# A two-layer hybrid block: shorter triangular inverse, silu in pieces, norm chains raised in priority, and instruction order from the scheduler's timeline model

## The chip, the cores and the metric

The kernel runs on one core of one Trainium2 chip, in one launch. The metric is the device time of an execution in microseconds (us). Runs of the kernel before took 1651.51, 1644.26 and 1647.09 us; the median is 1647.09 us.

## The reference, cut to what matters

Two layers work on 256 tokens of x and 256 tokens of ctx, 1024 wide. The second layer needs only x at its end.

```python
for l in range(DEPTH):                                  # DEPTH = 2
    mod_x = silu(c) @ w_mod[l] + b_mod[l]               # six shifts, scales, gates; same for ctx
    h_x = modulate(rms_norm(x, norm1_g[l]), sh1_x, sc1_x)
    y_x, y_c = hybrid_mixer(h_x, h_c, ...)              # three branches, then @ w_o
    x = x + gt1_x * y_x
    h_x = modulate(rms_norm(x, norm2_g[l]), sh2_x, sc2_x)
    x = x + gt2_x * conv_ffn(h_x, w_up[l], conv_ffn_w[l], w_down[l])
    # ctx the same, in layer 0 alone
```

The mixer's branches are a spatial gating unit (a), differential softmax attention (b) and a gated delta rule (c). The last one works on chunks of 64 tokens in both directions: it solves a unit lower triangular system per chunk and head, and then runs a scan over four chunks of ctx and four of x:

```python
u = triangular_solve(I + a, v * beta, lower=True)
w = triangular_solve(I + a, kb * exp(G), lower=True)
def step(state, blk):
    v_new = u_c - w_c @ state
    o_c   = qd_c @ state + in_c @ v_new
    state = state * gt_c + kt_c^T @ v_new
```

## The kernel before, in words

Activations lie transposed in SBUF, features on the partitions and 512 columns (ctx, then x) along the free side; in layer 1 most products take the 256 columns of x alone (`c0 = 256`). Every large product is made of three fp32r matmuls per 128 by 128 block of weights: a weight block comes in by a DMA on SyncE's queue (`wload`, L269, or `first_load`, L301), ScalarE rounds it to fp32r (`wh`, L237), VectorE takes the rest (`wl`, L219), and TensorE multiplies high by high, low by high and high by low (`mm3`, L240 is the matmul line of all helpers). Names in the profile are the outputs: `pqkv`, `ptm`, `pu`, `pj`, `pg`, `pbr`, `pwo`, `pup` and `pdn` are such products. `pu`, `ptm`, `pj`, `pg` and `pbr` are independent of the branches' small steps, and can stand between them.

The order of the program: `start` (the first modulation rows and the first norm), `norm_end` or `norm_halves` (norm and modulation into `hh` and `hl`), the mixer, its last product `wo` (`pwo`), a norm, the feed-forward layer (`pup`, `pdn`), a norm, and again for layer 1. I call the norm between `wo` and the feed-forward layer of layer 0 boundary B, that between the layers boundary C, and the one before the last feed-forward layer boundary D. `norm_halves` treats x and then ctx: sums of squares (`pss`), a reciprocal root of ten small VectorE steps (`rsqv`, `rs`, `rsqt`), its broadcast by TensorE (`pb`), and for eight blocks a product `xn`, then `hh` on ScalarE and `hl` on VectorE. The other modulation rows are made beside all this by `mod` (L467): 80 DMAs of 512 KB (`wmt`, L478), one or two VectorE products with a sum each (`mj` and `wmt`, L483), by the silu of the condition `scb` (one ScalarE step over 2048 columns); `more` (L490) issues the next of them at fixed points of the layer's code.

Branch c: `gdn_solve` (L1210) inverts 32 by 32 blocks on VectorE in 31 steps of two operations (`sT`, `sL`), transposes the result twice (`sLC`, and `sLR` by way of a ScalarE copy `sLt`), makes the off-diagonal parts on TensorE (`pZ`, `pU`, tiles of 32 rows), and ScalarE copies all into `U` (L1257, L1279), which VectorE then scales. `gdn_step` (L1285) is one scan step: `pkS` (state times keys), `rhs` on VectorE, `pV` (times U), `vn` on VectorE in one or two forms, `pq` and `pgo` where an output is wanted, `pS`, and four times two `gS` updates on VectorE, from which the next `pkS` starts. These matmuls use 64 rows or 64 columns of the array. `gdn_out` turns the result (`pgT`) and VectorE multiplies it into `z`. Branch a: `pj` and a gelu give `gv`, which `pmix` multiplies by the gating weights `sguwb`, loaded on ScalarE's queue (L734). Branch b: scores `psc`, a softmax, `paT` (transposes), a copy `aT`, `po`, a norm of `on` after four heads, `poT`.

What order the instructions stand in on each engine is not written out: a list scheduler of the framework takes the program's operations with priorities (`tc.high_priority(offset=AHEAD)` raises them) and a model of the machine's timing, and gives each engine its queue, which runs strictly in that order.

Of the kernel before, what the change touches and what calls it, by code (L numbers as in the profile page):

```python
# [173 lines left out]
class _Kernel:  # L174
# [175 lines left out]

    def run(self):
        nc = self.nc
        self.ahead, self.late, self.alt = {}, [], 0
        xf, N = self.start()
        xsrc = self.a["xT"]
        for l in range(L):
            last = l == L - 1
            if l > 0:
                self.load_par(l)
            hh, hl = self.norm_halves(N) if last else self.norm_end(N, self.first)  # L360
            c0 = 256 if last else 0
            if not last:
                self.mods = self.mod()
            xf, N = self.mixer(l, hh, hl, xsrc, c0)
            hh, hl = self.norm_end(N) if last else self.norm_halves(N)
            N = self.ffn(l, hh, hl, xf, c0)
            if not last:
                xsrc = self.dp.tile([128, 8, NT], F32, tag="xs", name="xs")
                for j in range(2):
                    nc.scalar.dma_start(out=xsrc[:, 4 * j:4 * j + 4], in_=xf.t[j])  # L370
        for m0, m1 in ((0, 4), (4, 6), (6, 7), (7, 8)):
            nc.sync.dma_start(out=self.out[:, m0:m1], in_=xf.t[m0 // 4][:, m0 % 4:(m1 - 1) % 4 + 1, 256:512])
# [94 lines left out]
    def mod(self):  # L467


        nc = self.nc  # L470
        sb = self.cp.tile([128, 2, 1024], F32, tag="scb", name="scb")
        nc.sync.dma_start(out=sb, in_=self.a["cB"])
        self.act(sb, sb, AF.Silu)
        for n in range(80):
            l, j = (0, 16 + n) if n < 32 else (1, n - 32)
            vs = (0, 1) if l == 0 or j < 16 else (1,)
            w = self.wp.tile([128, 1024], F32, tag="wm", name="wmt", bufs=1)
            nc.sync.dma_start(out=w, in_=self.a["wmt"][n])  # L478
            if n % 4 == 0:
                m4 = self.small("m4", [128, 4, 2], bufs=2)  # L480
            for v in vs:
                o = w if v else self.tmp("mj", [128, 1024], BF16)
                nc.vector.scalar_tensor_tensor(out=o, in0=w, scalar=1.0, in1=sb[:, v], op0=ALU.mult, op1=ALU.mult,  # L483
                                               accum_out=m4[:, n % 4, v:v + 1])
            if n % 4 == 3:
                self.add(self.modv[l][:, j - 3:j + 1, vs[0]:], m4[:, :, vs[0]:],
                         self.P(l, "bmod", j - 3, 4).unsqueeze(2).to_broadcast([128, 4, len(vs)]))
            yield

    def more(self, n=1):  # L490
        for _ in range(n):
            next(self.mods, None)

    def mod_first(self, order):
        for g, h in order:
# [43 lines left out]
    def norm_halves(self, N):  # L539
# [6 lines left out]
        for v, cs in ((1, slice(256, 512)), (0, slice(0, 256))):  # L546
# [7 lines left out]
            for k in range(8):  # L554
                self.mul(xn[:, k, cs], xn[:, k, cs], pb[:, cs])
                sh = mv[:, s + k, v:v + 1]
                self.act(hh[:, k, cs], xn[:, k, cs], AF.Identity, bias=sh)
                self.stt(hl[:, k, cs], xn[:, k, cs], sh, hh[:, k, cs].bitcast(F32), ALU.add, ALU.subtract)
        self.rest = iter(())
        return hh, hl  # L560

# [67 lines left out]
    def mixer(self, l, hh, hl, xsrc, c0):  # L629
# [32 lines left out]
        if c0 == 0:  # L662
            p = [self.bank("pg"[m % 2], "pwo") for m in (6, 7)]
            w = [self.tiles(self.a["wo"][l, m], 0, 8) for m in (6, 7)]
            for i, v in self.ends(p, w, _Two(yh), _Two(yl)):
                self.resid(l, 16, 6 + i, xf, p[i], 0, 0.5, (v,))
                self.norm_add(N, 6 + i, v)
        return xf, N

    def resid(self, l, s, m, xf, p, c0, scale, vs=None):  # L670
# [539 lines left out]
    def gdn_solve(self, g):  # L1210
# [18 lines left out]
            self.sub(Lm[:, j + 1:, :m], Lm[:, j + 1:, :m], tv)  # L1229
        LC = self.tp.tile([128, 32, 32], F32, tag="t4a", name="sLC", bufs=1)  # L1230
        nc.vector.transpose(LC.rearrange("p i t -> p (i t)"), Lf)
        Lt = self.tp.tile([128, 32, 32], F32, tag="t4c", name="sLt", bufs=1)
        self.act(Lt, Lm.rearrange("p i c -> p c i"), AF.Copy)
        LR = self.tp.tile([128, 32, 32], F32, tag="t4b", name="sLR", bufs=1)
        nc.vector.transpose(LR.rearrange("p i t -> p (i t)"), Lt.rearrange("p c i -> p (c i)"))
        Z = self.tp.tile([128, 32, 32], F32, tag="t4c", name="sZ", bufs=1)
        Af = A.rearrange("p f t y -> p f (t y)")
        for hb in range(2):
            pz = self.bank("g", "pZ")
# [12 lines left out]
        for a in range(2):  # L1252
            for y in range(2):
                src = LCv if a == y else LRv
                for b in range(2):
                    r = slice(64 * a + 32 * b, 64 * a + 32 * b + 32)
                    self.act(U[r, :, y, :, 32 * b:32 * b + 32], src[r, :, y], AF.Copy)  # L1257
                b = 1 if a == y else 0
                r = slice(64 * a + 32 * b, 64 * a + 32 * b + 32)
                nc.gpsimd.memset(U[r, :, y, :, 32 - 32 * b:64 - 32 * b], 0.0)  # L1260
        for hb in range(2):
# [13 lines left out]
            for a in range(2):  # L1275
                for y in range(2):
                    b = 0 if a == y else 1
                    r = slice(64 * a + 32 * b, 64 * a + 32 * b + 32)
                    self.act(U[r, 2 * hb:2 * hb + 2, y, :, 32 - 32 * b:64 - 32 * b], pv[r, :, y], AF.Copy)  # L1279
        for t in range(4):  # L1280
            Ut = U[:, t].rearrange("p y h i -> p (y h) i")
            self.mul(Ut, Ut, g["r1"][:, t].unsqueeze(2).to_broadcast([128, 8, 64]))
# [88 lines left out]
    def ffn(self, l, hh, hl, xf, c0):  # L1371
        nc = self.nc
        n = NT - c0
        for hf in range(2):
# [49 lines left out]
            if ps:  # L1424
# [2 lines left out]
                    w[i] += self.tiles(self.a["wdn"][l, hf, 6 + i][:, k0:k0 + kn].rearrange("p k m -> p (k m)"), k0, kn)  # L1427
                fht, flt = _Two(fh), _Two(fl)
                for i, v in self.ends(ps, w, fht, flt):
                    self.resid(l, 40, 6 + i, xf, ps[i], 0, 1.0, (v,))  # L1430
                    self.norm_add(N, 6 + i, v)
        return N if l + 1 < L else None


# [25 lines left out]
```

## Time and profile before

| | us |
|---|---|
| median of three runs | 1647.09 |
| the profiled execution | 1642.39 |
| its span, first to last instruction | 1640.6 |
| TensorE busy | 1583.4 |
| VectorE busy | 1207.0 |
| ScalarE busy | 767.9 |

The profiled execution is 1.8 us longer than its span, and 4.7 us (0.3%) under the median of the runs. "Busy" adds the time in which an engine ran at least one instruction; a pipelined engine can be busy and still deliver less than it could. The granted clock is TensorE's, 1.00 for its upper level.

### The profile page before, as it was taken

What the parts mean: (1) busy time and instruction counts of PE and PEld (TensorE: products, weight loads), DVE (VectorE), ACT (ScalarE), POOL (GpSimd) and SP (SyncE); (2) the same over time, 40 slices, a digit from 0 to 9 for tenths busy, and PEclk for the clock granted to TensorE, in tenths of its full rate; (3) what the DMA queues carried; (4) which work ended last, traced back from release to release, by engine and by line L of the source; (5) the groups of instructions that cost most, each with busy time, mean ns of one, the idle gap of its engine ahead of it and who ended that gap; (6) DMA issues with size and microseconds to landing.
All of it is one profiled execution on the core that took longest, in us unless ns stands there. A gap on an engine that the chain in (4) does not pass through costs nothing.

```text
span 1640.6 us, 27599 instructions
## 1 busy us (share of the span) xinstructions
PE 1583.4 (97%) x10664; PEld 1346.9 (82%) x10664; DVE 1207.0 (74%) x2831; ACT 767.9 (47%) x1455; POOL 6.6 (0%) x16
## 2 busy tenths in 40 slices
PE   5999999999999998999999999999999999989999
PEld 3777977876788887888888887888878799989998
DVE  5649977788764457999778876659777776788685
ACT  3654461156532333544234443654723754556563
POOL 0000000000000000000000000000000000000000
PEclk9999989999999998999999999999999999989999
DMA  8313321142343433454566565221222246545655
GB/s 340 132 60 110 107 66 53 65 125 69 100 145 94 150 93 101 128 171 160 166 203 201 191 195 182 78 92 53 70 64 83 86 144 223 186 132 180 191 181 154
DMA packets 65283, 218.22 MB, mean 133 GB/s; under 512 B 7552, under 2 KB 13696, under 8 KB 63232
## 3 DMA queue, kind: packets, MB, share of 16 engines
q1 hardware_dynamic: 63280, 208.70, 39.9%
q10 hardware_dynamic: 1872, 7.77, 1.3%
q8 instruction: 83, 1.36, 0.3%
q14 instruction: 48, 0.39, 0.1%
HBM read 213.29 MB, written 3.15 MB: 132 GB/s over the span
## 4 chain that ended last, share of the span: by engine, by line
PE 83%; DVE 7%; ACT 4%; DMA 2%; issue 2%; ACTq 0%; DVEq 0%
PE pup L240 21%; PE pg L240 12%; PE pdn L240 10%; PE pqkv L240 7%; PE pbr L240 6%; PE ptm L240 4%; PE pwo L240 4%; PE pu L240 2%; PE psc L240 2%; PE pj L240 2%; PE pS L240 2%; ACT U L237 1%; DMA wmt<-in_wmt_dram 1%; PE pkS L240 1%; PE po L240 1%
## 5 line engine op out<-in xcount | busy, mean ns | idle before, releaser
L237 ACT ACTIVATE wh<-wr 128x512 fp32r<-128x512 f32 (+1 forms) x594 | 366.7, 622 | 432.1 <-PE pdn L240 91.1
L219 DVE TENSOR_TENSOR wl<-wr,wh 128x512 fp32r<-128x512 f32 (+1 forms) x592 | 399.4, 680 | 156.8 <-ACT wh L237 154.1
L240 PE MATMUL pup<-hh,wh 128*128 128x256 f32 (+1 forms) x720 | 242.3, 337 | 2.2 <-ACT hh L237 2.1
L240 PE MATMUL pup<-hh,wl 128*128 128x256 f32 (+1 forms) x720 | 241.4, 336 | 0.0
L240 PE MATMUL pup<-hl,wh 128*128 128x256 f32 (+1 forms) x720 | 240.3, 335 | 0.0
L240 PEld LDWEIGHTS pup<-hh,wh 128*128 128x128 f32 x720 | 139.1, 193 | 16.8 <-ACT hh L237 2.9
L240 PEld LDWEIGHTS pup<-hh,wl 128*128 128x128 f32 x720 | 139.1, 193 | 13.0
L240 PEld LDWEIGHTS pup<-hl,wh 128*128 128x128 f32 x720 | 138.4, 193 | 13.1
L240 PE MATMUL pg<-hh,wh 128*128 128x512 f32 (+1 forms) x384 | 131.0, 341 | 0.1
L240 PE MATMUL pg<-hh,wl 128*128 128x512 f32 (+1 forms) x384 | 130.4, 339 | 0.2 <-DVE wl L219 0.2
L240 PE MATMUL pg<-hl,wh 128*128 128x512 f32 (+1 forms) x384 | 130.2, 339 | 0.0
L240 PE MATMUL ptm<-wh,hl 128*128 128x256 f32 x448 | 130.2, 291 | 0.0
L240 PE MATMUL ptm<-wl,hh 128*128 128x256 f32 x448 | 129.6, 289 | 0.3 <-DVE wl L219 0.3
L240 PE MATMUL ptm<-wh,hh 128*128 128x256 f32 x448 | 129.4, 289 | 0.0
L234 DVE SCALAR_TENSOR_TENSOR fcv<-pup,par,fcv 128x510 f32<-128x510 f32 (+1 forms) x176 | 107.3, 612 | 26.2 <-ACT fcv L237 26.1
L240 PE MATMUL pdn<-fh,wh 128*128 128x256 f32 (+1 forms) x366 | 121.0, 330 | 0.7 <-ACT fh L237 0.7
L240 PE MATMUL pdn<-fl,wh 128*128 128x256 f32 (+1 forms) x366 | 120.6, 330 | 0.7 <-DVE fl L219 0.7
L240 PE MATMUL pdn<-fh,wl 128*128 128x256 f32 (+1 forms) x366 | 120.7, 330 | 0.0
L483 DVE SCALAR_TENSOR_TENSOR wmt<-wmt,scb 128x1024 f32<-128x1024 f32 x80 | 97.7, 1221 | 23.1 <-DMA wmt<-in_wmt_dram 22.6
L240 PEld LDWEIGHTS ptm<-wh,hh 128*128 128x128 f32 x448 | 86.6, 193 | 2.7 <-issue 2.0
L240 PEld LDWEIGHTS ptm<-wl,hh 128*128 128x128 f32 x448 | 86.6, 193 | 2.5 <-issue 1.7
L240 PEld LDWEIGHTS ptm<-wh,hl 128*128 128x128 f32 x448 | 86.7, 194 | 2.1 <-issue 1.7
(332 smaller groups left out, 3223.1 us busy)
## 6 DMA issues: line engine op xcount, KB each, us to landing
wmt<-in_wmt_dram SPq DMA_DIRECT2D x80, 512.0 KB, 3.6
wr<-in_wup_dram SPq DMA_DIRECT2D x80, 512.0 KB, 3.9
wr<-in_wfm_dram SPq DMA_DIRECT2D x78, 512.0 KB, 3.5
wr<-in_wtm_dram SPq DMA_DIRECT2D x32, 512.0 KB, 3.6
wr<-in_wdn_dram SPq DMA_DIRECT2D x32, 512.0 KB, 3.9
wr<-in_wbr_dram SPq DMA_DIRECT2D x24, 512.0 KB, 3.6
wm<-in_wmod_dram SPq DMA_DIRECT2D x8, 1024.0 KB, 11.0
wr<-in_wo_dram SPq DMA_DIRECT2D x16, 512.0 KB, 3.5
```

The source lines that it names most:

```text
L219: self.nc.vector.tensor_tensor(out=out, in0=a, in1=b, op=op)
L234: self.nc.vector.scalar_tensor_tensor(out=out, in0=a, scalar=s, in1=b, op0=op0, op1=op1)
L237: self.nc.scalar.activation(out, a, f, bias=bias, scale=scale, **k)
L240: self.nc.tensor.matmul(out, lhsT, rhs, start=start, stop=stop, **k)
L483: nc.vector.scalar_tensor_tensor(out=o, in0=w, scalar=1.0, in1=sb[:, v], op0=ALU.mult, op1=ALU.mult, accum_out=m4[:, n % 4, v:v + 1])
```

## The change

- The scheduler is told to work with its other model of the machine (`schedule_with_timeline_sim=True`), so that the order on every engine is made anew.
- `norm_halves` and the residual and norm sums of the last two output blocks of `wo` and of `pdn` are raised in priority; the `wmt` products that `more` issues after a `norm_halves` are told to issue after its last `hl`.
- The silu of `scb` is made in four pieces of 512 columns.
- In the solve the copy `sLt` is dropped and `sLR` is transposed straight from the strided view of `sL`; half of the copies into `U` go from ScalarE to VectorE.

```diff
--- before.py
+++ after.py
@@ -350,19 +350,27 @@
 
     def run(self):
         nc = self.nc
-        self.ahead, self.late, self.alt = {}, [], 0
+        self.ahead, self.late, self.alt, self.after = {}, [], 0, None
         xf, N = self.start()
         xsrc = self.a["xT"]
         for l in range(L):
             last = l == L - 1
             if l > 0:
                 self.load_par(l)
-            hh, hl = self.norm_halves(N) if last else self.norm_end(N, self.first)
+            if last:
+                with self.tc.high_priority(offset=AHEAD):
+                    hh, hl = self.norm_halves(N)
+            else:
+                hh, hl = self.norm_end(N, self.first)
             c0 = 256 if last else 0
             if not last:
                 self.mods = self.mod()
             xf, N = self.mixer(l, hh, hl, xsrc, c0)
-            hh, hl = self.norm_end(N) if last else self.norm_halves(N)
+            if last:
+                hh, hl = self.norm_end(N)
+            else:
+                with self.tc.high_priority(offset=AHEAD):
+                    hh, hl = self.norm_halves(N)
             N = self.ffn(l, hh, hl, xf, c0)
             if not last:
                 xsrc = self.dp.tile([128, 8, NT], F32, tag="xs", name="xs")
@@ -470,7 +478,10 @@
         nc = self.nc
         sb = self.cp.tile([128, 2, 1024], F32, tag="scb", name="scb")
         nc.sync.dma_start(out=sb, in_=self.a["cB"])
-        self.act(sb, sb, AF.Silu)
+        for v in range(2):
+            for i in range(2):
+                s = sb[:, v, 512 * i:512 * i + 512]
+                self.act(s, s, AF.Silu)
         for n in range(80):
             l, j = (0, 16 + n) if n < 32 else (1, n - 32)
             vs = (0, 1) if l == 0 or j < 16 else (1,)
@@ -488,8 +499,9 @@
             yield
 
     def more(self, n=1):
-        for _ in range(n):
-            next(self.mods, None)
+        with self.tc.issue_after(self.after) if self.after is not None else ExitStack():
+            for _ in range(n):
+                next(self.mods, None)
 
     def mod_first(self, order):
         for g, h in order:
@@ -555,7 +567,9 @@
                 self.mul(xn[:, k, cs], xn[:, k, cs], pb[:, cs])
                 sh = mv[:, s + k, v:v + 1]
                 self.act(hh[:, k, cs], xn[:, k, cs], AF.Identity, bias=sh)
-                self.stt(hl[:, k, cs], xn[:, k, cs], sh, hh[:, k, cs].bitcast(F32), ALU.add, ALU.subtract)
+                self.after = self.nc.vector.scalar_tensor_tensor(
+                    out=hl[:, k, cs], in0=xn[:, k, cs], scalar=sh, in1=hh[:, k, cs].bitcast(F32), op0=ALU.add,
+                    op1=ALU.subtract).ins
         self.rest = iter(())
         return hh, hl
 
@@ -663,8 +677,9 @@
             p = [self.bank("pg"[m % 2], "pwo") for m in (6, 7)]
             w = [self.tiles(self.a["wo"][l, m], 0, 8) for m in (6, 7)]
             for i, v in self.ends(p, w, _Two(yh), _Two(yl)):
-                self.resid(l, 16, 6 + i, xf, p[i], 0, 0.5, (v,))
-                self.norm_add(N, 6 + i, v)
+                with self.tc.high_priority(offset=AHEAD):
+                    self.resid(l, 16, 6 + i, xf, p[i], 0, 0.5, (v,))
+                    self.norm_add(N, 6 + i, v)
         return xf, N
 
     def resid(self, l, s, m, xf, p, c0, scale, vs=None):
@@ -1229,11 +1244,9 @@
             self.sub(Lm[:, j + 1:, :m], Lm[:, j + 1:, :m], tv)
         LC = self.tp.tile([128, 32, 32], F32, tag="t4a", name="sLC", bufs=1)
         nc.vector.transpose(LC.rearrange("p i t -> p (i t)"), Lf)
-        Lt = self.tp.tile([128, 32, 32], F32, tag="t4c", name="sLt", bufs=1)
-        self.act(Lt, Lm.rearrange("p i c -> p c i"), AF.Copy)
-        LR = self.tp.tile([128, 32, 32], F32, tag="t4b", name="sLR", bufs=1)
-        nc.vector.transpose(LR.rearrange("p i t -> p (i t)"), Lt.rearrange("p c i -> p (c i)"))
-        Z = self.tp.tile([128, 32, 32], F32, tag="t4c", name="sZ", bufs=1)
+        LR = self.tp.tile([128, 32, 32], F32, tag="t4c", name="sLR", bufs=1)
+        nc.vector.transpose(LR, Lm.rearrange("p i c -> p c i"))
+        Z = self.tp.tile([128, 32, 32], F32, tag="t4b", name="sZ", bufs=1)
         Af = A.rearrange("p f t y -> p f (t y)")
         for hb in range(2):
             pz = self.bank("g", "pZ")
@@ -1254,7 +1267,10 @@
                 src = LCv if a == y else LRv
                 for b in range(2):
                     r = slice(64 * a + 32 * b, 64 * a + 32 * b + 32)
-                    self.act(U[r, :, y, :, 32 * b:32 * b + 32], src[r, :, y], AF.Copy)
+                    if b == 0:
+                        self.act(U[r, :, y, :, 0:32], src[r, :, y], AF.Copy)
+                    else:
+                        nc.vector.tensor_copy(U[r, :, y, :, 32:64], src[r, :, y])
                 b = 1 if a == y else 0
                 r = slice(64 * a + 32 * b, 64 * a + 32 * b + 32)
                 nc.gpsimd.memset(U[r, :, y, :, 32 - 32 * b:64 - 32 * b], 0.0)
@@ -1276,7 +1292,10 @@
                 for y in range(2):
                     b = 0 if a == y else 1
                     r = slice(64 * a + 32 * b, 64 * a + 32 * b + 32)
-                    self.act(U[r, 2 * hb:2 * hb + 2, y, :, 32 - 32 * b:64 - 32 * b], pv[r, :, y], AF.Copy)
+                    if a == 0:
+                        self.act(U[r, 2 * hb:2 * hb + 2, y, :, 32 - 32 * b:64 - 32 * b], pv[r, :, y], AF.Copy)
+                    else:
+                        nc.vector.tensor_copy(U[r, 2 * hb:2 * hb + 2, y, :, 32 - 32 * b:64 - 32 * b], pv[r, :, y])
         for t in range(4):
             Ut = U[:, t].rearrange("p y h i -> p (y h) i")
             self.mul(Ut, Ut, g["r1"][:, t].unsqueeze(2).to_broadcast([128, 8, 64]))
@@ -1427,8 +1446,9 @@
                     w[i] += self.tiles(self.a["wdn"][l, hf, 6 + i][:, k0:k0 + kn].rearrange("p k m -> p (k m)"), k0, kn)
                 fht, flt = _Two(fh), _Two(fl)
                 for i, v in self.ends(ps, w, fht, flt):
-                    self.resid(l, 40, 6 + i, xf, ps[i], 0, 1.0, (v,))
-                    self.norm_add(N, 6 + i, v)
+                    with self.tc.high_priority(offset=AHEAD):
+                        self.resid(l, 40, 6 + i, xf, ps[i], 0, 1.0, (v,))
+                        self.norm_add(N, 6 + i, v)
         return N if l + 1 < L else None
 
 
@@ -1452,7 +1472,7 @@
         arrays[f"in_{n}_dram"] = v
         aps[n] = nc.dram_tensor(f"in_{n}_dram", v.shape, mybir.dt.from_np(v.dtype), kind="ExternalInput").ap()
     out = nc.dram_tensor("out_0_dram", (128, 8, SEQ), F32, kind="ExternalOutput").ap()
-    with tile.TileContext(nc) as tc:
+    with tile.TileContext(nc, schedule_with_timeline_sim=True) as tc:
         body(tc, aps, out)
     r = run_bass_kernel_spmd(nc, [arrays], core_ids=[0])
     y = np.asarray(r.results[0]["out_0_dram"])
```

What the new order does shows at three places. The first is TensorE's queue in the second half of layer 0's scan: `ptm` are matmuls of a large product that nothing in the scan waits for, the others belong to a scan step. Before:

```order
L240 MATMUL pV_2885<-rhs_2880,U_1312 64x128 x4
L240 MATMUL pq_2897<-gS_2466,qT_616 64x128 x7
L240 MATMUL ptm1_3226<-wh_3233,hh_124 128x256
L240 MATMUL ptm1_3226<-wh_3233,hl_125 128x256
L240 MATMUL ptm1_3226<-wl_3234,hh_124 128x256
L240 MATMUL ptm1_3226<-wh_3229,hh_124 128x256
L240 MATMUL ptm1_3226<-wh_3229,hl_125 128x256
L240 MATMUL ptm1_3226<-wl_3230,hh_124 128x256
L240 MATMUL ptm1_3226<-wh_3229,hh_124 128x256
L240 MATMUL pgo_2906<-vn_2894,inT_1043 64x128 x8
L240 MATMUL pS_2919<-vn_2894,ktok_1041 128x128 x4
L240 MATMUL pS_2928<-vn_2894,ktok_1041 128x128 x4
```

And the steps of the changed kernel at the same place:

```order
L240 MATMUL ptm1_3381<-wl_3447,hh_124 128x256
L240 MATMUL pkS_2742<-gS_2467,kT_188 64x128 x8
L240 MATMUL pV_2756<-rhs_2751,U_1310 64x128 x2
L240 MATMUL pq_2768<-gS_2467,qT_616 64x128 x8
L240 MATMUL pV_2756<-rhs_2751,U_1310 64x128 x6
L240 MATMUL pgo_2777<-vn_2765,inT_1043 64x128 x8
L240 MATMUL pS_2789<-vn_2765,ktok_1041 128x128 x4
L240 MATMUL pS_2798<-vn_2765,ktok_1041 128x128 x4
L240 MATMUL pkS_2807<-gS_2467,kT_188 64x128 x8
L240 MATMUL pV_2821<-rhs_2816,U_1310 64x128 x2
L240 MATMUL pq_2833<-gS_2467,qT_616 64x128 x8
L240 MATMUL pV_2821<-rhs_2816,U_1310 64x128 x6
```

Before, each part of a step has matmuls of `ptm` (or of `pu`) behind it in the queue; now the four last steps of layer 0 (from `pkS_2742` on) follow each other with none between them, and so do, but for 22 matmuls of `pj` in the last, five of layer 1.

The second place is TensorE's queue at the end of branch b and the output of branch c in layer 0 (`pgT` turns a result of the scan; `pbr` and `pg` are matmuls of large products). Before:

```order
L1362 MATMUL pgT_4807<-cst0_77,go_2488 128x128 x4
L240 MATMUL pbr_4613<-yal_4304,wh_4605 128x512
L240 MATMUL pbr_4613<-yah_4303,wh_4605 128x512
L240 MATMUL pbr_4613<-yah_4303,wl_4606 128x512
L240 MATMUL pbr_4613<-yal_4304,wh_4605 128x512
L240 MATMUL pg_4627<-hh_124,wh_4630 128x512
L240 MATMUL pg_4627<-hh_124,wl_4631 128x512
L240 MATMUL pg_4627<-hl_125,wh_4630 128x512
L240 MATMUL pg_4627<-hh_124,wh_4630 128x512
L240 MATMUL pg_4627<-hh_124,wl_4631 128x512
L240 MATMUL pg_4627<-hl_125,wh_4630 128x512
L1362 MATMUL pgT_4816<-cst0_77,go_2546 128x128 x4
```

And now:

```order
L922 MATMUL paT_4239<-cst0_77,pr_4222 128x128 x4
L240 MATMUL po_4246<-vB_1413,aT_4244 128x128 x4
L922 MATMUL paT_4270<-cst0_77,pr_4253 128x128 x4
L240 MATMUL po_4277<-vB_1413,aT_4275 128x128 x4
L937 MATMUL poT_4298<-cst0_77,on_4159 128x128 x4
L1381 MATMUL pgT_4808<-cst0_77,go_2489 128x128 x4
L1381 MATMUL pgT_4817<-cst0_77,go_2547 128x128 x4
L1381 MATMUL pgT_4826<-cst0_77,go_2786 128x128 x4
L1381 MATMUL pgT_4835<-cst0_77,go_2851 128x128 x4
L240 MATMUL pbr_4906<-ych_4844,wh_4898 128x512
```

The `pbr` and `pg` that stood between the last `paT`, `po`, `poT` and the four `pgT` stand elsewhere now (earlier, or behind the last `pgT`).

The third place is VectorE's queue at boundary B (`rsqv`, `rs` and `rsqt` are the reciprocal root, `mj` and `wmt` the modulation products). Before:

```order
L219 TENSOR_TENSOR rsqt_6229<-rs_6225 128x2
L483 SCALAR_TENSOR_TENSOR mj_6507,m4_6506<-wmt_6504,scb_1417 128x1024
L219 TENSOR_TENSOR rsqt_6229<-rsqt_6229,rsqv_6228 128x2
L231 TENSOR_SCALAR rsqv_6267<-pss_6223 128x2
L234 SCALAR_TENSOR_TENSOR rsqt_6229<-rsqt_6229 128x2
L483 SCALAR_TENSOR_TENSOR wmt_6504,m4_6506<-wmt_6504,scb_1417 128x1024
L234 SCALAR_TENSOR_TENSOR rs_6225<-rsqt_6229,rs_6225 128x2
L231 TENSOR_SCALAR rs_6225<-rsqv_6267 128x2
L219 TENSOR_TENSOR rsqt_6229<-rs_6225 128x2
L219 TENSOR_TENSOR rsqt_6268<-rs_6225 128x2
```

And now:

```order
L234 SCALAR_TENSOR_TENSOR rsqt_6269<-rsqt_6269 128x2
L570 SCALAR_TENSOR_TENSOR hl_5831<-xn_5828,modv0_90,hh_5830 128x256 x3
L234 SCALAR_TENSOR_TENSOR rs_6226<-rsqt_6269,rs_6226 128x2
L219 TENSOR_TENSOR rsqt_6269<-rs_6226 128x2
L234 SCALAR_TENSOR_TENSOR rsqt_6269<-rsqt_6269,rsqv_6268 128x2
L234 SCALAR_TENSOR_TENSOR rs_6226<-rsqt_6269,rs_6226 128x2
L219 TENSOR_TENSOR xn_5827<-xn_5827,pb_6225 128x256 x4
L219 TENSOR_TENSOR xn_5828<-xn_5828,pb_6225 128x256 x4
L570 SCALAR_TENSOR_TENSOR hl_5831<-xn_5827,modv0_90,hh_5830 128x256 x4
L570 SCALAR_TENSOR_TENSOR hl_5831<-xn_5828,modv0_90,hh_5830 128x256 x4
L494 SCALAR_TENSOR_TENSOR mj_6508,m4_6507<-wmt_6505,scb_1415 128x1024
L494 SCALAR_TENSOR_TENSOR wmt_6505,m4_6507<-wmt_6505,scb_1415 128x1024
```

The modulation products stood within the reciprocal root; they now stand behind the last `hl` of both halves.

## Rows read from the trace of the kernel before

**Rows 1.** The page: the span, and the engines' busy time with the share of the span.
```profile
span 1640.6 us, 27599 instructions
...
PE 1583.4 (97%) x10664; PEld 1346.9 (82%) x10664; DVE 1207.0 (74%) x2831; ACT 767.9 (47%) x1455; POOL 6.6 (0%) x16
```
**Rows 2.** Windows: stretch, length, each engine's busy time, granted clock, DMA share, GB/s.
```profile
13.00:60.00 47.00, 41.71 (x319) 28.47 (x320) 31.60 (x85) 19.65 (x33) 0.00 (x0) 1.00 0.74 290
155.00:205.00 50.00, 49.06 (x402) 47.87 (x401) 49.87 (x176) 20.93 (x36) 0.00 (x0) 1.00 0.36 109
240.00:320.00 80.00, 80.00 (x719) 60.93 (x719) 60.25 (x181) 12.08 (x21) 1.13 (x2) 1.00 0.18 57
428.00:452.00 24.00, 23.90 (x125) 18.70 (x123) 21.08 (x57) 12.33 (x29) 0.00 (x0) 1.00 0.36 110
...
650.00:655.00 5.00, 3.95 (x17) 3.65 (x18) 4.25 (x14) 2.43 (x6) 0.00 (x0) 0.50 0.36 110
```
**Rows 3.** TensorE's waits: what waited for what, us in total, times, longest us.
```profile
PE pss L240 <- DVE sqs L219: 19.0, 4, 13.5
...
PE pgram L240 <- ACT U L237: 3.2, 1, 3.2
```
**Rows 4.** Timeline of TensorE in a scan step of layer 1: start, length, operation.
```profile
1202.88 1.71 PE L240 MATMUL pS<-vn,ktok 64*128 64x128 f32 x16
...
1206.85 0.65 PE L240 MATMUL pkS<-gS,kT 128*64 128x128 f32 x6
1207.43 0.39 PE L240 MATMUL pu<-hh,wl 128*128 128x256 f32 x1
1207.65 0.28 PE L240 MATMUL pu<-hl,wh 128*128 128x256 f32 x1
1207.77 0.28 PE L240 MATMUL pu<-hh,wh 128*128 128x256 f32 x1
...
1209.59 0.65 PE L240 MATMUL pV<-rhs,U 64*64 64x128 f32 x8
```
**Rows 5.** Timeline of VectorE in the same scan step.
```profile
1204.08 2.16 DVE L234 SCALAR_TENSOR_TENSOR gS<-gS,g_gts,pS 128x128 f32<-128x128 f32 x8 [0.18 <-PE pS L240]
...
1207.54 1.13 DVE L234 SCALAR_TENSOR_TENSOR rhs<-pkS,g_neG,vtok 128x128 f32<-128x128 f32 x4 [0.63 <-PE pkS L240]
...
1210.29 0.69 DVE L219 TENSOR_TENSOR vn<-pV,g_tail 128x512 f32<-128x512 f32 x1 [0.95 <-PE pV L240]
```
**Rows 6.** The ACT copy before `sLR`, all of it (count, ns min/median/max, first and last start).
```profile
L237 ACT ACTIVATE sLt<-sL x2: 2085/2110/2134, 205.2 to 1162.4; 128x1024 f32<-128x1024 f32 x2
```
**Rows 7.** The page: VectorE's second parts of weights, and its modulation products (mean ns).
```profile
L219 DVE TENSOR_TENSOR wl<-wr,wh 128x512 fp32r<-128x512 f32 (+1 forms) x592 | 399.4, 680 | 156.8 <-ACT wh L237 154.1
...
L483 DVE SCALAR_TENSOR_TENSOR wmt<-wmt,scb 128x1024 f32<-128x1024 f32 x80 | 97.7, 1221 | 23.1 <-DMA wmt<-in_wmt_dram 22.6
```
**Rows 8.** The load of `sguwb` (layers 0 and 1): all of it, and its time to landing.
```profile
L734 ACTq DMA_DIRECT2D sguwb<-in_sguw_dram x2: 339/340/340, 316.1 to 1257.4; - x2
...
DMA to landing us min/median/max: 2.6/2.8/2.9
```
**Rows 9.** The chain of waits, 428 to 470 us: start, length, what.
```profile
437.81 0.29 ACT on L237
...
440.34 0.70 DVE on L219
...
445.90 2.09 PE pg L240 x9
```
**Rows 10.** Timeline of VectorE, end of the attention branch in layer 0.
```profile
443.84 1.12 DVE L234 SCALAR_TENSOR_TENSOR z<-pgT,par,z 128x128 f32<-128x128 f32 x4
```
**Rows 11.** Timeline at boundary B.
```profile
648.03 1.22 DVE L483 SCALAR_TENSOR_TENSOR wmt<-wmt,scb 128x1024 f32<-128x1024 f32 x1
...
649.98 1.22 PE L240 MATMUL pb<-cst,rs 128*128 128x128 f32 x4 [2.27 <-DVE rs L234]
```

## The prediction

> **What bounds the kernel now.** I read the page first: TensorE is busy for 1583.4 of 1640.6 us [rows 1], so no other engine is a bound for long: little can be won, and whatever uncovers TensorE is lost. Then I read the windows: from 240 to 320 us, the scan of layer 0, TensorE is busy all of 80.00 us at the full clock [rows 2], although a scan step is a chain through two engines. What covers the chain are the matmuls of `ptm` and `pu` that stand between its parts. From 155 to 205 us, the solve of layer 0, VectorE is busy 49.87 and TensorE 49.06 of 50 us: both are full, and VectorE sets the end. From 428 to 452 us, the end of the attention branch, TensorE is busy 23.90 of 24 us. Third, the waits: TensorE waits 19.0 us in four pieces for the norms' sums, 13.5 of them at the start, and 3.2 us for the copies into `U` [rows 3]. So before, the order of the queues hides nearly every chain, and the change makes that order anew. What counts is where a chain has lost its cover.
>
> **The change, part by part**, against the profiled execution of 1642.39 us.
>
> *Array shapes.* TensorE changes between 128 by 128 and the scan's 64-wide tiles. After `pkS` a `pu` takes 0.22 us to the next, and that one 0.12 [rows 4]: 0.10 us for one change. In the order of the queue they fall from 373 to 243, so 130 x 0.10 = 13 us less (8 to 20, as a change costs something on either side or not).
>
> *Scans.* This is the largest term. A bare step without output goes: `pS` to the first `gS` 1204.08 - 1202.88 = 1.20 us, `gS` 2.16, the last `pkS` 0.65, `rhs` 1.13, the last `pV` 0.65, `vn` 0.69 [rows 4, 5], together 6.5 us. TensorE's own work in it is `pS` 1.64 (1.71 less the overlap), `pkS` 1.0 and `pV` 1.2, 3.8 us: 2.7 us idle. With an output, `vn` comes a second time (0.6), and `pq` and `pgo` take 1.0 us each: 9.0 us against 5.8, 3.2 idle. In the new order the last four steps of layer 0 and five of layer 1 (two without output) stand bare: 4 x 3.2 and 2 x 2.7 + 3 x 3.2, less 1.5 for the 22 `pj` in the last, is 12.8 + 13.5 = 26 us. Below: nothing, if VectorE's part overlaps more than I see; above: 9 x 4 = 36.
>
> *End of attention.* Before, the chain `po`, copy `on`, root, `on`, `poT` runs from 437.81 to 441.04 us, and the `pgT` that follow wait for `z`, 1.12 us each [rows 9, 10]; some 65 `pg` and `pbr` stand between, 9 of which take 2.09 us [rows 9], so about 15 us of cover. Now none stands from the last but one `paT` to the `pbr` behind `pgT`. Uncovered are the 3.3 us before `poT`, three times a `z`, and the copies and the softmax between `paT` and `po`, which no row shows bare. Below, that is 3.3 + 3 x 1.12 and two copies of at least 0.29 each, 7 us; above, all of the cover, 15 us. I take 14, since before TensorE ran through the stretch with just this cover [rows 2]. In layer 1 two `pgT` lose theirs: 4 us (0 to 5).
>
> *Solve.* Ahead of `sLC` VectorE has more to do than before: 7 modulation products of 1.15 us (1.221 less an overlap of 0.07), 7 `wl` of 0.60, and parts of the attention's norms and softmax, 9 us [rows 7]: 21 us. Ahead of `pZ` TensorE has 16 us more: 48 `pu` x 0.23, and `psc`, `pqkT` and `ptm`. As VectorE was full there [rows 2], `pZ` comes 21 us later, of which 16 are filled. The dropped copy `sLt` of 2.11 us [rows 6] ran beside the first transpose, so `sLR` gains 0.6. That leaves 21 - 16 - 0.6 = 4 us in layer 0, and by the same count (21 against 18) 2 in layer 1. But the new queues also mix the solve's steps with what TensorE waits for singly, and then nothing is covered: 21 each. I take 9 each, nearer the lower ends since TensorE has its work in the queue: 18 us.
>
> *Copies into U.* They are now on two engines, which shortens the 3.2 us wait [rows 3], but the `pu` that stood there are gone: -2 us (-6 to +4).
>
> *Behind the scans.* `pmix` needs `sguwb`, whose load is issued when the last `gS` is done (316.1 us) and lands after 2.8 us [rows 8]. Before, `ptm` and `pj` stood there; now `pmix` follows the last `pS` of layer 0. From `pS`, 1.2 + 2.2 + 0.3 + 2.8 us, less its own 1.6, is 5 us; in layer 1 a norm in front of the second `pmix` is less covered, 3 us. Together 8 (0 to 14).
>
> *Norms.* At B the two modulation products, 1.22 us each, leave the chain in which TensorE waits 2.27 us for `rs` [rows 11], but all `xn` come before the first `hl`: -2 us; C -1 us (together -5 to +2). The products move behind `hl` into the feed-forward layer, beside that layer's own VectorE work: 3 us (0 to 10, eight products of 1.15 us).
>
> *Start.* The DMAs are busy 0.74 of 13 to 60 us [rows 2]; `scb` (1 MB), `par`, `cst` and `wmt` now go ahead of three weight blocks on SyncE's queue: +4 us (0 to 8). The silu in pieces costs ScalarE under 1 us beside other work: 0.
>
> *Clock.* After the waits of boundary B the granted clock was 0.50, the lower of the two levels, while matmuls already ran [rows 2]. The uncovered stretches of the attention and of the two solves should bring that too: half of some 5 us each, 3 x 2.5 = 8 us (0 to 40, with the scans). The Trainium skill, "TensorE: Matmul & The Clock Gate", Part 1, says that the throttled state is the default and that activity releases it. The row agrees, and by that rule every stretch with idle gaps is at risk, the bare scans too; nine of them at the lower level would make the sum 36 us larger (rival 1).
>
> Sum: -13 + 26 + 18 + 18 - 2 + 8 - 3 + 3 + 4 + 8 = +67 us, 1709.4 us by the profiled execution. That one lies 4.7 us under the median of the runs shown, so I say **1714 us**.
>
> **Rivals.**
> 1. *Bare chains at the lower clock* (chance 0.17). In the bare scans TensorE works only 60% of the time. If the clock falls there as at B, its share of each step (about 4 us on the chain) doubles: 9 x 4 = 36 us more, 1750 us. For it: 0.50 after B. Against it: a pause between its parts is under 2 us, and from 13 to 60 us the clock stayed at 1.00 with TensorE busy 41.71 of 47 us.
> 2. *Only the scans and the attention lose* (0.20): the solve's VectorE work finds its cover, the clock and the start stay as they are, `sguwb` lands in time, and the feed-forward layer hides the products. 67 - 18 - 8 - 4 - 8 - 3 = 26 us: 1673 us.
> 3. *No difference* (0.05): steps of different chains overlap, so that of the lost cover in scans, attention, solve, behind the scans and at the start a third counts: (26 + 18 + 18 + 8 + 4) / 3 = 25 us, against 18 of gains, 1654 us.
> 4. *Faster* (0.04). The uncovered places count nothing, because VectorE runs ahead: its queue holds fewer other steps in the bare stretches, so that a step falls to TensorE's own work. It decides below 6 us for a step with output; then only -13 - 2 - 3 are left: 1629 us.
>
> **How the numbers follow.** Slower stands on three independent places with lost cover, each of more than 10 us, against some 30 us of gains at their upper ends: forecast 0.54 and rivals 1 and 2 make 0.91. A measurement of this kernel tells about 0.5%, 8 us, from no change: slower 0.91, same 0.05, faster 0.04. The range reaches from rival 2 with a smaller scan term, 1662, to rival 1, 1755 us; beyond lie rivals 3 and 4 and the largest clock costs.
>
> **What would show it.** In the trace after: TensorE idle for VectorE (`gS`, `rhs`, `vn`) some 3 us in each of nine scan steps; 10 us or more between `po` and the `pbr` behind the last `pgT` of layer 0; `pmix` waiting for a DMA; `pZ` of layer 0 25 to 30 us later than the end of VectorE's full stretch at 205; no modulation product between `pss` and the last `hl` at B. The prediction is wrong if TensorE stays busy through the scans' last steps, or if its busy time is lost in the feed-forward layers, for which I expect next to nothing.

## The result, and the profile after

The changed kernel takes 1753.62 us (median of 1753.87, 1746.83, 1753.38 and 1761.32), the kernel before beside it 1645.99 us: ratio 1.0646, 95% interval [1.0617, 1.0674]. It is slower by 107.6 us, on the forecast's side and 1.4 us short of the upper end of its range; the sum of 67 us was too small.

The page after answers to [rows 1] and [rows 7]:

```profile
span 1752.1 us, 27619 instructions
PE 1606.6 (92%) x10664; PEld 1372.0 (78%) x10664; DVE 1225.1 (70%) x2847; ACT 741.2 (42%) x1436; POOL 7.7 (0%) x16
L494 DVE SCALAR_TENSOR_TENSOR wmt<-wmt,scb 128x1024 f32<-128x1024 f32 x80 | 97.6, 1220 | 36.9 <-DMA wmt<-in_wmt_dram 36.7
```

The same number of matmuls runs in a span that is 111.5 us longer: TensorE is busy 23 us more and idle 88 us more. VectorE has 18 us more work but now sits idle 36.9 us ahead of `wmt`, for its load, against 23.1 before. The granted clock, in the cores' view of before and then of after:

```profile
core 0: 1640.6 us, clock 0.985
```

```profile
core 0: 1752.1 us, clock 0.952
```

With levels of 1.00 and 0.50, that is 0.015 x 1640.6 x 2 = 49 us at the lower level before and 168 us after. Next the windows of after by stage: the first products; solve, copies into `U` and scan of layer 0; the end of the attention; the feed-forward layer of layer 0; solve and scan of layer 1 (columns as in [rows 2]).

```profile
20.00:89.50 69.50, 61.21 (x389) 42.59 (x387) 37.47 (x86) 31.29 (x60) 0.00 (x0) 0.93 0.50 184
171.70:247.00 75.30, 65.02 (x452) 60.51 (x450) 70.08 (x229) 28.23 (x50) 0.00 (x0) 0.92 0.36 112
247.00:268.00 21.00, 16.53 (x342) 13.58 (x342) 13.12 (x26) 11.76 (x21) 2.53 (x4) 0.50 0.01 2
268.00:365.80 97.80, 85.83 (x850) 72.62 (x848) 62.09 (x177) 15.06 (x25) 1.11 (x2) 0.97 0.11 34
507.10:535.60 28.50, 15.72 (x63) 11.72 (x63) 14.93 (x44) 9.59 (x24) 0.00 (x0) 0.59 0.06 18
717.60:1093.40 375.80, 360.98 (x1630) 294.76 (x1628) 279.10 (x496) 139.09 (x241) 0.00 (x0) 1.00 0.50 157
1210.80:1270.90 60.10, 51.39 (x362) 47.39 (x360) 56.25 (x171) 24.54 (x42) 0.00 (x0) 0.91 0.29 89
1288.70:1370.80 82.10, 69.00 (x686) 58.81 (x686) 48.09 (x126) 15.02 (x27) 0.00 (x0) 0.94 0.15 46
```

Before, TensorE was full in the solves, the scans, the end of the attention and the feed-forward layer (83.03 of 83.20 us in the scan of layer 0), all at 1.00. The feed-forward layer of layer 0 before:

```profile
662.20:1016.70 354.50, 353.79 (x1616) 294.64 (x1615) 287.09 (x511) 143.97 (x240) 0.00 (x0) 1.00 0.56 179
```

Stages that trade independent matmuls can't be compared by length, so I add up what each loses: for every matmul, the time to the next one's start beyond the lower quartile of that time for the same form in the trace of before. Half clock, idle time and shape changes are all in it. The level of a stage depends on how finely forms are told apart; its difference between two kernels hardly does, and only differences are used here.

| stage | before | after | more | forecast |
|---|---|---|---|---|
| first products | 10.8 | 24.5 | 13.7 | 4 |
| both solves | 4.3 | 29.9 | 25.6 | 18 |
| copies into `U` | 17.2 | 19.8 | 2.6 | -2 |
| both scans, without the wait for `pmix` | 26.7 | 42.6 | 15.9 | 26 - 13 |
| behind the scans, with that wait of 6.2 | 3.2 | 20.3 | 17.1 | 8 |
| end of attention | 3.6 | 29.1 | 25.5 | 18 |
| boundaries B and C | 16.2 | 17.7 | 1.5 | -3 |
| feed-forward layer of layer 0 | 2.5 | 22.2 | 19.7 | 3 |
| all else | 51.1 | 41.0 | -10.1 | 0 |
| clock | | | (in the rows above) | 8 |

The sum is 111.5 us, the difference of the spans. The clock has no row of its own, but it can be estimated. At the end of the attention (below) nine `pg` take 3.82 us at the lower level, 2.09 at the upper [rows 9], so 45% of TensorE's busy time there is the clock's. In the whole trace it was busy for some 40 us at the lower level before and some 131 us after: about 41 of the 111.5 us, spread over the rows. TensorE's longest waits in the whole of after:

```profile
PE pss L240 <- DVE sqs L219: 19.4, 4, 13.4
PE pgo L240 <- DVE vn L219: 8.9, 6, 1.5
PE pup L240 <- DVE wl L219: 8.8, 9, 1.8
PE pmix L240 <- DVE go L219: 6.2, 1, 6.2
PE psq L240 <- ACT sse L237: 6.1, 1, 6.1
PE pV L240 <- DVE rhs L234: 6.0, 9, 1.6
PE pgT L1381 <- DVE z L234: 5.8, 4, 1.8
PE pkS L240 <- DVE gS L234: 5.8, 8, 0.9
PE pu L240 <- ACT axq L237: 5.7, 2, 3.1
PE pdn L240 <- DVE wl L219: 5.0, 5, 1.8
```

Before, no wait but that of `pss` came to more than 5.2 us in total. No single wait has replaced another: the loss is spread over many of 1 to 6 us. The wait of `pmix` is put down to `go`, but it ends with the load of `sguwb`, issued at 369.0 us and landed 2.8 to 3.1 us later; `pmix` starts at 372.01 (in the run with the second buffer, below, the trace names the load itself, 6.0 us):

```profile
L749 ACTq DMA_DIRECT2D sguwb<-in_sguw_dram x2: 340/340/340, 369.0 to 1372.8; - x2
```

Two places close up. A bare scan step of layer 0, on TensorE's timeline (answers to [rows 4]):

```profile
345.25 1.71 PE L240 MATMUL pS<-vn,ktok 64*128 64x128 f32 x16
347.88 1.22 PE L240 MATMUL pkS<-gS,kT 128*64 128x128 f32 x16 [0.92 <-DVE gS L234]
349.55 0.43 PE L240 MATMUL pV<-rhs,U 64*64 64x128 f32 x4 [0.46 <-DVE rhs L234]
349.92 1.09 PE L240 MATMUL pq<-gS,qT 128*64 128x128 f32 x16
350.94 0.87 PE L240 MATMUL pV<-rhs,U 64*64 64x128 f32 x12
353.30 1.09 PE L240 MATMUL pgo<-vn,inT 64*64 64x128 f32 x16 [1.48 <-DVE vn L219]
354.32 2.48 PE L240 MATMUL pS<-vn,ktok 64*128 64x128 f32 x16
```

From one `pS` to the next are 9.07 us (9.0 were forecast), 2.86 of them idle (3.2). And the chain of waits at the end of the attention in layer 0 (answers to [rows 9, 10]):

```profile
515.99 0.29 ACT on L237
...
519.25 1.13 PE poT L937 x4
...
526.50 1.10 PE pgT L1381 x4
527.60 0.03 issue
527.62 1.14 DVE z L234 x4
...
531.09 1.22 PE pbr L240 x2
532.31 3.82 PE pg L240 x9
```

Before, nothing of this chain showed as a wait; now TensorE takes 28.5 us for 15.7 us of busy time, at a mean clock of 0.59.

### The profile page after: what moved, and what is told of

It is laid out like the page before. It is cut to its first block, busy times and chain, and to the rows that moved or that the text cites. A ratio compares the mean times of both kernels' runs of the same rounds, so it can differ in the third digit from the quotient of the medians.

```text
span 1752.1 us, 27619 instructions
## 1 busy us (share of the span) xinstructions
PE 1606.6 (92%) x10664; PEld 1372.0 (78%) x10664; DVE 1225.1 (70%) x2847; ACT 741.2 (42%) x1436; POOL 7.7 (0%) x16
## 4 chain that ended last, share of the span: by engine, by line
PE 66%; DVE 14%; DMA 11%; issue 5%; ACT 3%; SPq 0%; DVEq 0%; ACTq 0%
PE pg L240 11%; DMA wmt<-in_wmt_dram 10%; PE pup L240 10%; PE pdn L240 7%; PE ptm L240 7%; PE pqkv L240 6%; PE pbr L240 6%; PE pwo L240 4%; DVE wmt L494 2%; PE pu L240 2%; PE pj L240 2%; PE psc L240 2%; DVE wl L219 1%; PE pV L240 1%; PE po L240 1%
## 5 line engine op out<-in xcount | busy, mean ns | idle before, releaser
L494 DVE SCALAR_TENSOR_TENSOR wmt<-wmt,scb 128x1024 f32<-128x1024 f32 x80 | 97.6, 1220 | 36.9 <-DMA wmt<-in_wmt_dram 36.7
```

## The experiments

**The model alone, and all but the model.**

```diff
-    with tile.TileContext(nc, schedule_with_timeline_sim=True) as tc:
+    with tile.TileContext(nc) as tc:
```

> All edits of the change but one: the scheduler keeps its default model of the machine. Theory (the order of the other model costs the time; the edits of the code cost nothing): the whole loss of about 107 us goes, 1640 us (1625 to 1655). Rival (the raised priorities and the products behind the last hl cost a good part, whatever the model): 1680 us or more. The mean granted clock should be back near 0.985 by the theory.

1641.64 us, 0.9968 [0.9952, 0.9984] of the kernel before, clock 0.983. The opposite, the kernel before with the other model alone:

> The kernel before with the scheduler's other model alone, no other edit. Theory: 1745 to 1775 us, as slow as the change or a little slower, because the norms' gain and the shorter solve are missing. Rival (model and edits share the loss): 1690 to 1725 us.

1760.44 us, 1.0708 [1.0653, 1.0764]. So the whole loss comes from the order by the other model, and by the method above at the same places (end of attention of layer 0: 21.7 us lost in both, feed-forward layer 22.0). The edits themselves gain a little: 0.3% with the default model. How the loss splits among the places is a matter of the next runs.

**A second buffer for `wmt`**, in the place where the forecast had expected next to nothing:

```diff
-            w = self.wp.tile([128, 1024], F32, tag="wm", name="wmt", bufs=1)
+            pool, tag = (self.tp, "t4a") if self.two and n % 2 else (self.wp, "wm")
+            w = pool.tile([128, 1024], F32, tag=tag, name="wmt", bufs=1)
```

(`self.two` is set in the feed-forward layer of layer 0.)

> The change, with a second buffer for wmt in the feed-forward layer of layer 0 (every other load goes into a 4 KB buffer of the solve that stands empty there). Theory (the 20 us lost in that layer come from modulation products at the head of VectorE's queue that wait for the load of their only buffer, so that wl behind them comes late): VectorE's waits for wmt fall from 37 us to under 15, TensorE's waits for wl in this layer go, 1754 becomes 1735 to 1742 us. Rival (wl is late for another reason, such as the order of the weights' own loads): within 4 us of 1754.

1736.12 us, as the theory had it. VectorE's waits in that layer, of the change (717 to 1093 us):

```profile
DVE wmt L494 <- DMA wmt<-in_wmt_dram: 30.7, 22, 2.9
DVE mj L494 <- DMA wmt<-in_wmt_dram: 28.6, 22, 3.3
```

and with the second buffer:

```profile
DVE wmt L498 <- DMA wmt<-in_wmt_dram: 14.9, 15, 2.3
```

TensorE's waits for `wl` there were 8.8 us (`pup`) and 5.0 us (`pdn`) in the change; they fall to 0.6 and to

```profile
PE pdn L240 <- DVE wl L219: 1.6, 1, 1.6
```

`mj` is not among VectorE's longest waits any more (in the whole run the waits for `wmt` fall from 36.9 to 22.0 us, not to under 15), and the loss of the layer falls from 22.2 to 9.2 us. The first products lose 6 less here and the scan of layer 0 5 more, with the same order of the loads: so far do these stages vary. In the first products the clock goes with it, 0.93 in the change and 1.00 here:

```profile
20.00:84.60 64.60, 55.93 (x376) 39.43 (x376) 37.12 (x86) 31.34 (x60) 0.00 (x0) 1.00 0.54 198
```

The load is issued when the last product has released the buffer and lands 3.6 us later; the new order puts the next product at the head of VectorE's queue before that, and `wl` behind it is late for `pup` and `pdn`. Before, VectorE waited for `wmt` too (22.6 and 18.7 us there), but TensorE for no `wl`.

**The loads at the start.** SyncE's queue in the change, with `par`, `cst`, `scb` and the first `wmt` between these two:

```profile
16.19 2.34 SPq L456 DMA_DIRECT2D wm<-in_wmod_dram  x4
...
27.09 17.96 SPq L301 DMA_DIRECT2D wr<-in_wfm_dram  x6
```

The edit puts what stands between the first two `wm` and the `wr` behind the last weight load that is issued ahead:

```diff
-        self.load_par(0, nc.sync)
+        with self.tc.issue_after(self.lastw):
+            self.load_par(0, nc.sync)
...
```

> The change, with par, cst, scb, the first wmt and the last two wm loads put behind the weight blocks of the first products on SyncE's queue. Theory (the 14 us more that the first products lose come from 3.2 MB of loads that go ahead of those weights): the first products end 9 to 14 us earlier, 1740 to 1746 us. Rival (the first products wait for VectorE and ScalarE, or the later loads are missed elsewhere): within 5 us of 1754.

1747.69 us, ratio 1.0629 [1.0584, 1.0673], which overlaps the change's interval. The first products lose 18.3 us at a clock of 1.00, with the change's order of loads 18.4 (the second buffer's run, 1.00) to 24.5 (the change, 0.93), and 10.8 before. So the theory isn't borne out: at the same clock the order of the loads makes no difference that shows. Of the 7.5 us that remain, 3.5 are one wait: `psq` waits 6.1 us for ScalarE's `sse` in this run as in the change, 2.6 before. The rest stays open, and so does why the clock falls there in some of these runs.

**The solve.** The modulation products are issued behind the instruction that `self.after` names:

```diff
-        nc.vector.transpose(LC.rearrange("p i t -> p (i t)"), Lf)
+        t = nc.vector.transpose(LC.rearrange("p i t -> p (i t)"), Lf)
+        if self.l == 0:
+            self.after = t.ins
```

> The change, with the modulation products of layer 0's mixer put behind sLC on VectorE's queue, so that none stands within the solve. Theory (the solve of layer 0 ends late because VectorE has more to do ahead of sLC, 8 us of it in seven such products): pZ of layer 0 starts 8 us earlier or more, 1754 becomes 1744 to 1749 us, if the products find room beside the scan. Rival (the products only move the loss into the scan, whose chain VectorE sets as well): pZ earlier, the total within 4 us of 1754.

1740.72 us (1.0584 [1.0542, 1.0627]), 13 less, more than expected; the end of its interval just reaches the change's. `pZ` starts at 230.2 instead of 247.0 us, and the solve loses 3.6 instead of 15.9 us; the scan behind it loses 7 us more, where products now stand. The edit takes away not only the seven of the forecast: from 127 us up to `pZ` 20 products stood there, 24 us of VectorE, and 13 of them stood there before the change too. So taking the products away undoes most of this solve's loss, and part of it moves on; that the seven alone caused it is not shown.

**The end of the attention.**

```diff
-            self.proj_fm(self.a["wfm"][l, 20 + 8 * i + m], 8, self.hh, self.hl, c0, pg)
+            with self.tc.issue_after(self.po) if i == 0 and m > 5 else ExitStack():
+                self.proj_fm(self.a["wfm"][l, 20 + 8 * i + m], 8, self.hh, self.hl, c0, pg)
```

(and likewise for `pbr`; `self.po` is the last matmul of `po`.)

> The change, with the last two of eight output blocks of branch a (pg and pbr, 72 matmuls and some 15 us of TensorE's time in layer 0, half that in layer 1) put behind the last po on TensorE's queue. Theory (the end of the attention branch lost its cover, 20 us in layer 0 and 6 in layer 1): TensorE's idle time there falls by 10 to 15 and by 4 us, 1754 becomes 1735 to 1742 us. Rival (those matmuls covered the attention's earlier steps and are missed there): within 5 us of 1754.

1744.07 us (1.0588 [1.0541, 1.0635]), 10 less, short of the theory's range; the interval overlaps the change's, so the gain as a whole is barely clear of noise. The profiled execution took 1750.05 us, the slowest of the four. At the place the theory holds: the end of the attention loses 5.1 instead of 21.7 us in layer 0, 1.3 instead of 7.4 in layer 1. But in that execution most of it comes back as the rival has it: the attention's earlier steps of layer 0 lose 16.3 instead of 5.7 us, and the scan of layer 1 10.7 more.

**The scan.** `behind` returns `issue_after` of the last `pS`, `pkS` or `pV` of the step that a block of `ptm` is dealt to:

```diff
-                        self.mm(o, self.hh[:, k, xs], wh[j][:, ws], start=f, stop=False, skip_group_check=True)
...
+                        with self.behind(g, kb, i, tt, kk, c0):
+                            self.mm(o, self.hh[:, k, xs], wh[j][:, ws], start=f, stop=False, skip_group_check=True)
```

> The change, with ptm of branch a dealt out over the scan's steps: in layer 0 24 matmuls for each step from the second on (12 behind pS, 9 or so behind the next pkS, the rest behind pV), in layer 1 24 for each of the last four. Nothing is added or left out. Theory (a bare step loses about 3 us, a covered one nothing): four steps of layer 0 and four of layer 1 get cover and pmix of layer 0 still waits, 12 to 20 us less, 1734 to 1742 us. Rival (cover is worth the same wherever it stands, so that the early steps lose what the late ones gain): within 5 us of 1754.

1729.78 us, 24 less, more than expected. The scans lose 33.5 instead of 48.8 us, with the wait for `pmix`; the rest was won at the end of the attention (5 us) and in the first products (3 us, within their variation).

**All five together.**

> The change with the second wmt buffer, the later loads at the start, the products behind sLC, the attention's cover and the dealt out ptm together. Theory (separate places, so that the gains add up): 18 for the second buffer and 6 for the start as measured, 5, 14 and 14 for the others, 57 us: 1697 us (1685 to 1712). Rival (the places share one stock of independent matmuls, so that cover given to one is taken from another): 1715 us or more.

1707.93 us: within the theory's range, but that range was added up from smaller gains. The single gains add to 17.5 + 5.9 + 12.9 + 9.6 + 23.8 = 70 us; 46 came. That fits places that draw on one stock of independent matmuls, as the rival says, though not to its full extent. The other 62 us of the loss were not won back by any edit at a place; that they too belong to the order is shown by the first two runs alone.

**Bare steps in the kernel before**, a test from the other side:

```diff
+                es = ExitStack()
+                if g > 5:
+                    es.enter_context(self.tc.issue_after(self.pS))
                 for tt in range(2):
...
```

(`self.pS` is the scan's last `pS`, `g > 5` the `ptm` of branch a.)

> The kernel before (default model, none of the change's edits), with ptm of branch a put behind the last pS of the scan, so that the last two steps of each layer and half of the one ahead stand bare, with little but a few psc among them. Theory (a bare step loses some 3 us of TensorE's time, in any order): 5 bare steps x 3.2, less about 0.8 for the array's shape changes saved in each, is 12 us more: 1658 us (1652 to 1664). Rival (the step's chain costs little by itself, and the change's scans are slow for their VectorE queue, which holds more of other work): within 4 us of 1646.

1644.22 us, 0.9985 [0.9972, 0.9999]. The theory falls: steps whose only cover is a few `psc` cost nothing that shows here. Its timeline of TensorE in such a step of layer 0 suggests why:

```profile
302.82 1.71 PE L1342 MATMUL pS<-vn,ktok 64*128 64x128 f32 x16
304.94 0.43 PE L240 MATMUL pkS<-gS,kT 128*64 128x128 f32 x2 [0.41 <-DVE gS L234]
305.97 1.21 PE L240 MATMUL pkS<-gS,kT 128*64 128x128 f32 x14 [0.60 <-DVE gS L234]
307.62 0.44 PE L240 MATMUL pV<-rhs,U 64*64 64x128 f32 x4 [0.44 <-DVE rhs L234]
307.99 0.43 PE L240 MATMUL pq<-gS,qT 128*64 128x128 f32 x2
308.35 0.87 PE L240 MATMUL pV<-rhs,U 64*64 64x128 f32 x12
309.15 1.09 PE L240 MATMUL pq<-gS,qT 128*64 128x128 f32 x14
310.17 0.70 PE L240 MATMUL psc<-akT,qhT 64*128 64x256 f32 x4
310.80 1.09 PE L240 MATMUL pgo<-vn,inT 64*64 64x128 f32 x16
311.82 1.71 PE L1342 MATMUL pS<-vn,ktok 64*128 64x128 f32 x16
```

Here 14 of 16 `pq` stand behind the last `pV` and, with four `psc`, cover both forms of `vn`. In the change all 16 stand ahead of the last 12 `pV`, and TensorE waits 1.48 us for `vn`. From one `pS` to the next that step takes 9.0 us, 0.6 of them `psc`, so 8.4 of its own. A covered one of before, 302.8 to 314.1 us with 27 `ptm` of 0.12, takes 11.3 - 3.2 = 8.1 us beside its `ptm`; the change's bare step takes 9.07. So by these timelines cover in small pieces was worth little more than the shape changes that it brought, and `psc` and the order of `pq` and `pV` within the step are worth some 0.7 us. No run changed that order alone, so this reading is argued, not shown.

**Versions that beat both.** With the default model, the feed-forward layer of layer 0 still lost 11.9 us with all edits (2.5 before), while the copies into `U` lost 4.8 and 4.6 us (9.2 and 8.0) and B 4.3 (8.7). Three kernels, all with the default model: all edits and the second `wmt` buffer; all edits without the tie behind the last `hl`; the solve's edits alone.

> All edits of the change with the scheduler's default model, and the second wmt buffer in the feed-forward layer of layer 0. With the default model alone these edits gave 1641.6 us, with 12 us of TensorE's time lost in that layer against 2.5 before. Theory (the products tied behind the last hl are late there and wait for the load of their one buffer): 5 to 9 us less, 1632 to 1637 us, the fastest so far. Rival (the loss there is fh that comes late at the layer's middle, which the buffer doesn't touch): 1640 to 1643 us.

1635.71 us, 0.9931 [0.9913, 0.9949], the lowest median (its interval and those of the next two overlap a little); the layer's loss is 2.3 us again.

> All edits of the change with the scheduler's default model, but the modulation products are not tied behind the last hl. Theory (tying them costs some 9 us in the feed-forward layer and gives 2 to 4 at boundary B): 1634 to 1640 us. Rival (the tie gives at B what it costs later): 1641 us or more.

1639.26 us, 0.9953 [0.9936, 0.9970]. By time within its theory's range, but not by its reason: without the tie the layer still loses 10.7 us, and B 4.7. So the tie is neither what costs there nor what gains at B.

> The kernel before with the edits of the solve alone (no copy sLt, half of the copies into U on VectorE) and the default model. Theory (the copies into U are the edit that gains, 4.4 and 3.4 us in the two layers with all edits): 1637 to 1640 us against 1646 of the kernel before. Rival (they gain only together with the others): 1644 us or more.

1638.69 us, 0.9955 [0.9939, 0.9972]: the solve's edits alone gain as much as all of them, since what the norms' edits win at B (8.1 against 4.3 us) goes in the feed-forward layer.

## Why the prediction was right, and where its sum was not

- **Direction and cause.** Right: the first and second run show that the order does all of it. That lost cover is how it does so is shown for a part: solve, attention, scan and feed-forward layer each gained by an edit at the place, 46 us together, those of the solve and the attention near the noise. The signs came for the most part (2.86 us idle in a bare step, 15 us from `po` to `pbr`, `pmix` behind a DMA). Two went the other way: `pZ` of layer 0 came at 247.0 us and not by 235, and time was lost in the feed-forward layer, which the prediction names as a sign of being wrong.
- **The range.** That 1753.62 us lies within it is luck in part: its upper end, 1755, was taken from rival 1, whose condition did not come.
- **Clock**, 8 us: some 41 by the estimate above, and so the term most mis-sized. It was priced at 2.5 us for each of three stretches, but the lower level stood in the copies into `U` (0.50), behind the scans, at the start and in most of the end of the attention as well. The rows below hold its share.
- **End of attention**, 18 us: 25.5. The mechanism is as said. What was mis-sized is the clock: at 0.59 TensorE was busy 15.7 us there, some 13 of them at the lower level, for 7.0 us of work by the quartiles of the full clock, so some 6 to 9 of layer 0's 21.7 us are the lower level, where the forecast had 2.5 us a stretch.
- **Solves**, 18 us: 25.6, a little nearer the upper bound of 21 each than the lower ones. In layer 0 the modulation products have most to do with it: without all 20 of them `pZ` came 16.8 us earlier. For layer 1 no run was made.
- **Scans**, 26 less 13: net 15.9. The bare step was forecast well (9.0 us; 9.07). But the nearly bare steps put into the kernel before cost nothing that shows: "3.2 idle" holds for the change's order within the step, not for a bare step as such, and by its timeline a covered step was not free either.
- **Behind the scans**, 8 us: 17.1. The load of `sguwb` in layer 0 was forecast at 5 and took 6.2; the norm ahead of the second `pmix` of layer 1 (3.9) and its clock of 0.80 were not counted.
- **Feed-forward layer**, 3 us: 19.7. This is the step that failed in its mechanism. It priced the products by their own time beside VectorE's other work, and left out that a product at the head of the queue waits for its own load while `wl` stands behind it. [rows 7] had a hint: 22.6 us of waiting for `wmt` before, though then no TensorE wait followed from it.
- **Start**, 4 us: 13.7, of which some 6 come and go with the clock (0.93 or 1.00) and 3.5 are the wait for `sse`. The loads ahead of the weights, which the forecast priced, made no difference that shows.
- **Copies into `U`**, -2: 2.6 with this order, at a clock of 0.50; but -4.4 and -3.4 with the default model, as argued. **B and C**, -3: B gave 1.7, C cost 3.2.
- **Shape changes**, -13: TensorE's matmuls change shape 373 times in the trace before and 243 in the one after, as counted. What a change costs wasn't measured by itself.
- **Rival 1** gave nearly the time that came, 1750, for a reason that did not: in the scans the clock stayed at 0.97 and 0.94. What fell to the lower level were other stretches: the copies into `U` of layer 0 (0.50), the end of the attention (0.59, with single waits of up to 3.3 us), the place behind layer 1's scan (0.80, 3.9). The Trainium skill, "TensorE: Matmul & The Clock Gate", Part 1, takes the lower level for the default that activity lifts. The trace agrees with that at the end of the attention (0.59, TensorE busy 15.7 of 28.5 us) and less plainly in the copies (0.50, busy 16.53 of 21 us); the scans, with gaps of 0.5 to 1.5 us, stayed at 0.97 and 0.94.

## What to carry to other kernels

When a scheduler makes the order anew, count for each chain what stands behind its links in the queue, and for each product what its engine waits for at the head of the queue: a wait for a load there delays all that stands behind it. Independent matmuls are one stock; cover given to one chain is taken from another, so gains of single places need not add (70 us singly, 46 together). Try edits and a new order apart: here useful edits (0.3%, and 0.7% with a second buffer) were buried under an order that cost 7%.

## What the runs showed that I had not expected

The lower clock took about 168 us of the span after, 49 before, though TensorE was busy for 92% of it. And scan steps with hardly any cover, in the kernel before, cost no time that could be measured: 1644.22 against 1647.41 us.
